# The prompt's state products moved to the head of each block of short products

## The chip, the core and the metric

The kernel runs on one core of one Trainium2 chip. The metric is the device time of one execution in microseconds (us). Engines: PE multiplies matrices, DVE (VectorE) and ACT (ScalarE) work on elements, POOL (GpSimd) does a little arithmetic and issues DMAs, SP (SyncE) issues DMAs. Each engine takes its instructions from a queue of its own and waits on semaphores for the others.

## The reference, cut to what matters

One layer of a hybrid streaming encoder for 256 rows of a new stream and 128 rows (8 streams of 16) of running ones, all in float32: one long projection, a pooling branch, a state-space branch (SSD), gates, an output projection and an MLP. The change lies in the SSD branch, which runs over 8 groups g of 8 heads:

```python
xbc, new_conv = causal_conv(xbc, st_conv, conv_w, conv_b)        # x, B, C after a short convolution
def step(h, inp):                                                # one chunk
    cum = cumsum(dtc * A);  decay = exp(cum[t] - cum[s])  (s <= t)
    cb = einsum('btgn,bsgn->btsg', Cc, Bc)
    y = einsum('btsgr,bsgrp->btgrp', cb * decay, xdt)            # within the chunk
    y = y + einsum('btgn,bgrpn->btgrp', Cc, h) * exp(cum)        # from the carried state
    h = h * exp(last) + einsum('bsgn,bsgr,bsgrp->bgrpn', Bc, w_end, xdt)   # the new state
y = y + d_skip * xh
a_ssd = rmsnorm_per_group(y * silu(z)) * g
```

For the prompt the carried state is zero, so its new state h is one product of B with the weighted x (x times dt times w_end) over all 256 rows. That product is "the state product of the prompt" in what follows. `rmsnorm_per_group` needs the sum of squares of a whole group.

## The kernel before, in words

**Tiles.** Rows lie along the free dimension: 384 columns, of which 256 are prompt and 128 are sample. A projection unit is 128 output channels: 16 k-steps of three products of 128x384, made in `half` (two halves of 8 k-steps, each with one weight tile of 128x1024). The three products per k-step (`mm3`, L76 to L78) replace one float32 product: each operand is split into a rounded high half and a rest. L76 is high weight by high input, L77 high weight by low input, L78 low weight by high input. A weight tile is loaded by SP (`wfetch`), its high half `wh` is made on ACT (L68) and its low half `wl` on DVE (L69, `wsplit`). There are three buffers for each of the three.

**One round per group** (loop at L799) is ten projection units: B, C, x0, x1, x2, x3, z0, z1, z2, z3. On PE they run in this order. Two blocks of short products stand between them:

- the first block, behind x2 (L834 to L847): `t_trx` (six transpositions of x0 and x1, tile trx, L587), `t_cb` (C by B, tile cb), `t_trB` (three transpositions of B, tile trB, L571), then for the previous group's second pair of channel tiles `t_pp` (six products, the state product of the prompt, tile py or pp, L630), `t_yT` and `t_Y` (tile Y), then `t_yi` for the new pair (tile py, L595) and `t_su` in `state` (the sample's new state, tile su, L735);
- the second block, behind z3 (L871 to L879): `t_trx` of x2 and x3, `t_pp`, `t_yT`, `t_Y` of the first pair, `t_yi` of the second pair, `t_su`.

In group 0 the first block has no part of a previous group; after group 7 the second pair's remainder runs behind the first unit of gate_b (L805 to L809). So there are 15 blocks in which `t_pp` stands between other short products, and one, after the last group, in which it stands directly behind long products.

The six products of `t_pp` multiply the split B (`Bhl`) with the split weighted x (`xhl`), both of type fp32r, as are the long products. Transpositions, cb, Y and yi are float32. `t_pp` writes the left half of a PSUM tile, `t_yi` the right half of the same tile. That tile comes from the pool `psm` of two buffers, which also holds the outputs of the long projections; all other short products write tiles of the pool `pss` of six.

**What reads the short products.** `bside` makes Bhl from trB (ACT L643, DVE L644); `xside` makes xdt and xdw from trx (four DVE instructions, L673), yis (L680) and xhl (ACT L687, DVE L688); `mside` makes cbm from cb (L666); `final` copies the state out (ACT L753), adds Y to x (L759) and multiplies by z (L767). An x unit is evicted from PSUM at L529 (then convolved, L540, L544), a z unit at L856 (then silu on ACT, L857).

**Between z1 and z2**, from group 1 on, `finish(prev)` (L865) normalizes the previous group: `norm_bc` splits the sum of squares (ACT L161, DVE L162 `nl`), sums it over the channels with two products on PE (tile bc, L165 and L166), and DVE takes the reciprocal root from it (L168, then `newton`, L151 to L155), after which L780 scales four tiles and POOL stores them.

**What sets the order.** On PE the order of this stage is written out: `half` and `lump` chain every group of products behind the last one (`tc.issue_after`). The queues of DVE, ACT, SP and POOL are not written out. A planner lays them when the kernel is built: it goes by the data each instruction needs, by its own estimates of how long things take, and by the order of the program. So the queue of one engine can be laid differently when the order on another engine is changed.

Of the kernel before, what the change touches and what calls it, by code (L numbers as in the profile page):

```python
# [33 lines left out]
def build(ctx, tc, io):  # L34
# [15 lines left out]
    def mmtile(name):  # L50
        return psm.tile([P, 512], F32, tag="mm", name=name)

    def sstile(name):
        return pss.tile([P, 512], F32, tag="ss", name=name)

    def behind(ins):
        return nullcontext() if ins is None else tc.issue_after(ins.ins)
# [440 lines left out]
    def gate_b(nb, pool, tag, hook=None):  # L498
        o = three(f"pj_gb{nb}")
        n = NB * 256 if tag == "hs" else 1536  # L500
        t = pool.tile([P, n], F32, tag=tag, name=f"gbt{nb}")[:, :1536].rearrange("p (b n) -> p b n", b=3)

        def done(b):
            s.activation(t[:, b], o[b], AF.Sigmoid, scale=yx[:, b : b + 1])
            gp.dma_start(gb_scr[nb][:, b], t[:, b])

        moving(o, [(io["w_gb"][nb, kp], f"gb{nb}_{kp}") for kp in range(8)], xg, 0, done, hook=hook)

    with tc.tile_pool(name="phd", bufs=2, reuse_waits="tile") as pd, tc.tile_pool(
# [40 lines left out]
        def lump(fn):  # L550
            with behind(last[0]):
                last[0] = fn()
# [3 lines left out]

        def pload(S):
            S.hs = pd.tile([P, NB, 2 * P], F32, tag="hs", name=f"hs{S.nm}")
            sy.dma_start(S.hs, io["ssm"][S.qd])

        def cload(S):
            S.cbcs = []
            for q in range(2):
                cbc = pd.tile([P, 2, T], F32, tag="cbc", name=f"cbc{S.nm}_{q}")
                sy.dma_start(cbc, cum_scr[S.h0 + q * 2 : S.h0 + q * 2 + 2, :].partition_broadcast(P))
                S.cbcs.append(cbc)
# [15 lines left out]
        def t_trx(S):  # L582
            S.trs = []
            for j in S.js:
                tr = sstile(f"trx{S.g}_{j}")
                for b in range(3):
                    i = te.transpose(tr[:, b * P : b * P + P], S.D.xs[j][:, b * P : b * P + P], ident)  # L587
                S.trs.append(tr[:, :T].rearrange("p (b h q) -> p b h q", b=3, h=2))
            return i
# [14 lines left out]
        def t_yT(S):  # L604
            S.Ys = []
            for q in range(2):
                Y = sstile(f"Y{S.nm}_{q}")
                i = te.transpose(Y[:, TP:T], S.yis[:, q], ident)
                S.Ys.append(Y)
            return i  # L610

        def t_Y(S):
            for q, Y in enumerate(S.Ys):
                for sb, e0, c0, n in ((0, 0, 0, TP), (1, TP, P, P), (2, T, TP, P)):
                    for c in range(4):
                        i = te.matmul(
                            Y[c * 32 : c * 32 + 32, c0 : c0 + n],
                            S.xdt[:, q, sb, c * 32 : c * 32 + 32],
                            S.E[:, q * 2 + c // 2, e0 : e0 + n],
                            start=False,  # L620
                            stop=sb > 0,
                            skip_group_check=True,
                        )
            return i

        def t_pp(S, py):
            S.pp = py[:, :256]
            for b in range(2):
                for bl, xl in ((0, 0), (0, 1), (1, 0)):
                    i = te.matmul(  # L630
                        S.pp.rearrange("p (j n) -> p j n", j=2),
                        S.D.Bhl[:, bl, b, :],
                        S.xhl[:, xl, :, b, :],
                        start=b + bl + xl == 0,
                        stop=b + bl == 2,
                        skip_group_check=True,
                    )
            return i
# [61 lines left out]
        def eside(S, q):  # L700
            if q == 0:
                S.E = pd.tile([P, 4, 512], F32, tag="E", name=f"E{S.nm}", bufs=1)
            for hh in (q * 2, q * 2 + 1):
                ch = S.cbcs[q][:, hh % 2]
                s.activation(S.E[:, hh, P:TP], ch[:, P:TP], AF.Exp, bias=tok[:, 9, S.h0 + hh : S.h0 + hh + 1])
                for b, e0 in enumerate((0, TP, T)):
                    s.activation(
                        S.E[:, hh, e0 : e0 + P],
                        ch[:, b * P : b * P + P],
                        AF.Relu,  # L710
                        bias=tok[:, b, S.h0 + hh : S.h0 + hh + 1],
                        scale=-1.0,
                    )
            Eq = S.E[:, q * 2 : q * 2 + 2]
            s.activation(Eq[:, :, :P], Eq[:, :, :P], AF.Exp, scale=-1.0)
            s.activation(Eq[:, :, TP:], Eq[:, :, TP:], AF.Exp, scale=-1.0)
            v.tensor_tensor(Eq, Eq, S.D.cbm.unsqueeze(1).to_broadcast([P, 2, 512]), ALU.mult)

        def dside(S):
            v.tensor_tensor(  # L720
                S.hs.rearrange("p b (h q) -> p b h q", h=4),
                S.hs.rearrange("p b (h q) -> p b h q", h=4),
                decb[:, S.h0 : S.h0 + 4, :].rearrange("p h b -> p b h").unsqueeze(3).to_broadcast([P, NB, 4, 64]),
                ALU.mult,
            )
# [72 lines left out]
        prev = None  # L798
        for g in range(G + 1):  # L799
            if g == G:  # L800
                eside(prev.p[1], 0)
                eside(prev.p[1], 1)
                dside(prev.p[1])
                gate_b(0, pd, "hs")
                py = mmtile("pp_last")  # L805
                lump(lambda: t_pp(prev.p[1], py))
                lump(lambda: t_yT(prev.p[1]))
                lump(lambda: t_Y(prev.p[1]))
                state(prev.p[1])  # L809
                final(prev.p[1])  # L810
                gate_b(1, pd, "hs")
                finish(prev)
                break
            u0 = 17 + g * 10
            D = Pair()
            D.g = g
            D.p = [pair(D, jp) for jp in range(2)]
            D.xs, D.zs = [], []
            D.BT = conv(u0, 32 + g, "BT", 2)
            pload(D.p[0])  # L820
            if g:
                eside(prev.p[1], 0)
            D.CT = conv(u0 + 1, 40 + g, "CT", 2)
            if g:
                eside(prev.p[1], 1)
            D.xs.append(conv(u0 + 2, g * 4, "xs", 6))
            if g:
                dside(prev.p[1])
            cload(D.p[0])
            cside(D)  # L830
            D.xs.append(conv(u0 + 3, g * 4 + 1, "xs", 6))
            b2 = conv_in(u0 + 4, g * 4 + 2)
            S = D.p[0]
            lump(lambda: t_trx(S))  # L834
            lump(lambda: t_cb(D))
            lump(lambda: t_trB(D))
            bside(D)
            S.py = mmtile(f"py{S.nm}")
            if g:
                lump(lambda: t_pp(prev.p[1], S.py))  # L840
                lump(lambda: t_yT(prev.p[1]))
                lump(lambda: t_Y(prev.p[1]))
            lump(lambda: t_yi(S))
            xside(S)
            mside(D)
            if g:
                state(prev.p[1])  # L847
                final(prev.p[1])
            D.xs.append(taps(b2, g * 4 + 2, "xs", 6))
            D.xs.append(conv(u0 + 5, g * 4 + 3, "xs", 6))  # L850
            eside(S, 0)

            def zproj(j):
                ps = proj(in_units(u0 + 6 + j), xg, f"z{g}_{j}")
                z = pd.tile([P, T], F32, tag="zs", name=f"zs{g}_{j}", bufs=7)
                v.tensor_tensor(z, ps, rstd, ALU.mult)  # L856
                s.activation(z, z, AF.Silu)  # L857
                D.zs.append(z)

            zproj(0)  # L860
            pload(D.p[1])
            eside(S, 1)
            zproj(1)
            if g:
                finish(prev)  # L865
            zproj(2)
            dside(S)
            cload(D.p[1])
            zproj(3)
            S1 = D.p[1]  # L870
            lump(lambda: t_trx(S1))  # L871
            S1.py = mmtile(f"py{S1.nm}")
            lump(lambda: t_pp(S, S1.py))
            lump(lambda: t_yT(S))
            lump(lambda: t_Y(S))
            lump(lambda: t_yi(S1))
            xside(S1)
            state(S)
            final(S)  # L879
            prev = D  # L880
# [311 lines left out]
    with tc.tile_pool(name="phg", bufs=1, reuse_waits="tile") as pg, tc.tile_pool(  # L1192
# [9 lines left out]
        for c8 in range(NC):  # L1202
            hh = []
            for f8 in range(8):
                f = c8 * 8 + f8
# [167 lines left out]
```

## Time and profile before

| | |
|---|---|
| median of 3 runs | 2807.32 us (2806.77 to 2808.29) |
| profiled execution | 2807.07 us |
| its span, first to last instruction | 2804.9 us |
| PE busy | 2792.9 us (100%) |
| DVE busy | 1501.4 us (54%) |
| ACT busy | 1173.4 us (42%) |
| the groups' stage, from the first block to the last | about 483 to 1237 us of the span |

In rows of the profile, L77 is line 77 of the kernel, `py<-xhl,Bhl` an output and its inputs, x6 a count of instructions. In a timeline a row shows the start, the length and the engine, and in brackets how long the engine had been idle before and what released it. A product's length includes its way through the array, so products overlap: what one costs is read from start to start.

### The profile page before, as it was taken

The numbers are of one execution on the slowest core, as the hardware profiler recorded it, in microseconds if no ns is written. First come the engines' busy times: TensorE is split into PE (matmuls) and PEld (weight loads), VectorE is DVE, ScalarE is ACT, GpSimd is POOL, SyncE is SP. The second block draws the span as 40 slices with busy tenths as digits, with TensorE's granted clock in tenths as the row PEclk, the third lists the DMA queues.
The fourth block names the chain that finished last, engine by engine and source line by source line (L and its number), as shares of the span: only waits on it lengthen the run. The fifth ranks groups of instructions, "written<-read, shape, count | busy, mean of one in ns | idle before, by whom it ended". The sixth has DMA issues, their size and how long they took to land.

```text
span 2804.9 us, 38300 instructions
## 1 busy us (share of the span) xinstructions
PE 2792.9 (100%) x15271; PEld 2542.6 (91%) x15271; DVE 1501.4 (54%) x1979; ACT 1173.4 (42%) x1822; POOL 105.8 (4%) x143
## 2 busy tenths in 40 slices
PE   9999999999999999999999999999999999999998
PEld 8998889999999999988888888989899898989897
DVE  6575335677787778756333336434444444444446
ACT  5443225556565656544322235433233332323233
POOL 0000000001010101010000000000000000000000
PEclk9999999999999999999999999999999999999999
DMA  7444445556665566657544544443444443444443
GB/s 272 131 124 150 139 139 199 186 182 207 197 228 192 201 198 223 197 186 233 175 146 161 176 144 131 130 131 125 131 126 129 127 130 126 129 128 128 130 127 124
DMA packets 148355, 451.35 MB, mean 161 GB/s; under 512 B 18064, under 2 KB 49104, under 8 KB 143184
## 3 DMA queue, kind: packets, MB, share of 16 engines
q1 hardware_dynamic: 140048, 412.97, 45.9%
q0 software_dynamic: 8128, 35.93, 3.3%
q8 instruction: 120, 1.97, 0.3%
q14 instruction: 59, 0.48, 0.1%
HBM read 407.11 MB, written 41.72 MB: 160 GB/s over the span
## 4 chain that ended last, share of the span: by engine, by line
PE 98%; ACT 1%; DMA 0%; DVE 0%; issue 0%; SPq 0%; DVEq 0%; ACTq 0%
PE pj_up L77 6%; PE pj_up L78 6%; PE pj_up L76 6%; PE wd L120 6%; PE wd L118 6%; PE wd L119 6%; PE pj_x L76 5%; PE pj_x L78 4%; PE pj_x L77 4%; PE pj_z L76 3%; PE pj_z L77 3%; PE pj_z L78 3%; PE pj_sp L119 3%; PE pj_sp L120 3%; PE pj_sp L118 3%; PE pj_gb L118 2%
## 5 line engine op out<-in xcount | busy, mean ns | idle before, releaser
L77 PE MATMUL pj_up<-x1l,wh_up 128*128 128x384 f32 (+1 forms) x1032 | 343.9, 333 | 0.6 <-DVE x1l L1041 0.6
L76 PE MATMUL pj_up<-x1h,wh_up 128*128 128x384 f32 (+1 forms) x1032 | 344.0, 333 | 0.0
L78 PE MATMUL pj_up<-x1h,wl_up 128*128 128x384 f32 (+1 forms) x1032 | 343.9, 333 | 0.0
L120 PE MATMUL wd<-wh_wd,hl 128*128 128x512 f32 x762 | 296.6, 389 | 0.0
L119 PE MATMUL wd<-wl_wd,hh 128*128 128x512 f32 x762 | 296.6, 389 | 0.0
L118 PE MATMUL wd<-wh_wd,hh 128*128 128x512 f32 x762 | 296.3, 389 | 0.0
L69 DVE TENSOR_TENSOR wl_wd<-w_wd,wh_wd 128x1024 fp32r<-128x1024 f32 x127 | 155.7, 1226 | 261.9 <-ACT wh_wd L68 261.9
L68 ACT ACTIVATE wh_wd<-w_wd 128x1024 fp32r<-128x1024 f32 x127 | 134.8, 1061 | 350.8 <-PE wd L120 284.2
L68 ACT ACTIVATE wh_up<-w_up 128x1024 fp32r<-128x1024 f32 x126 | 133.7, 1061 | 322.1 <-PE pj_up L77 258.0
L69 DVE TENSOR_TENSOR wl_up<-w_up,wh_up 128x1024 fp32r<-128x1024 f32 x126 | 154.4, 1226 | 198.1 <-ACT wh_up L68 198.0
L76 PE MATMUL pj_x<-xgh,wh_x 128*128 128x384 f32 x768 | 258.2, 336 | 0.0
L77 PE MATMUL pj_x<-xgl,wh_x 128*128 128x384 f32 x768 | 256.6, 334 | 0.0
L78 PE MATMUL pj_x<-xgh,wl_x 128*128 128x384 f32 x768 | 256.6, 334 | 0.0
L77 PEld LDWEIGHTS pj_up<-x1l,wh_up 128*128 128x128 f32 x1032 | 193.8, 188 | 1.0 <-DVE x1l L1041 0.7
L76 PEld LDWEIGHTS pj_up<-x1h,wh_up 128*128 128x128 f32 x1032 | 193.7, 188 | 0.3
L78 PEld LDWEIGHTS pj_up<-x1h,wl_up 128*128 128x128 f32 x1032 | 193.8, 188 | 0.0
L78 PE MATMUL pj_z<-xgh,wl_z 128*128 128x384 f32 x512 | 171.0, 334 | 0.0
L76 PE MATMUL pj_z<-xgh,wh_z 128*128 128x384 f32 x512 | 171.0, 334 | 0.0
L77 PE MATMUL pj_z<-xgl,wh_z 128*128 128x384 f32 x512 | 171.0, 334 | 0.0
L120 PEld LDWEIGHTS wd<-wh_wd,hl 128*128 128x128 f32 x762 | 143.0, 188 | 29.8
L119 PEld LDWEIGHTS wd<-wl_wd,hh 128*128 128x128 f32 x762 | 143.0, 188 | 29.7
L118 PEld LDWEIGHTS wd<-wh_wd,hh 128*128 128x128 f32 x762 | 143.0, 188 | 29.4
(319 smaller groups left out, 5799.7 us busy)
## 6 DMA issues: line engine op xcount, KB each, us to landing
w_up<-w_up SPq DMA_DIRECT2D x128, 512.0 KB, 3.4
w_wd<-w_down SPq DMA_DIRECT2D x128, 512.0 KB, 3.4
w_x<-w_in SPq DMA_DIRECT2D x96, 512.0 KB, 3.8
w_z<-w_in SPq DMA_DIRECT2D x64, 512.0 KB, 3.9
w_sp<-w_ssd SPq DMA_DIRECT2D x64, 512.0 KB, 3.4
w_ga<-w_ga SPq DMA_DIRECT2D x32, 512.0 KB, 3.5
w_pp<-w_pp SPq DMA_DIRECT2D x32, 512.0 KB, 3.4
hs<-ssm SPq DMA_DIRECT2D x16, 1024.0 KB, 5.4
```

The source lines that it names most:

```text
L68: s.activation(h, w, AF.Copy)
L69: v.tensor_tensor(l, w, h.bitcast(F32), ALU.subtract)
L76: te.matmul(out, wh, xh, start=first, stop=False, **how)
L77: te.matmul(out, wh, xl, start=False, stop=False, **how)
L78: return te.matmul(out, wl, xh, start=False, stop=last, **how)
L118: te.matmul(o[b], mh, wh[:, c], start=k == 0, stop=False)
L119: te.matmul(o[b], mh, wl[:, c], start=False, stop=False)
L120: last[0] = te.matmul(o[b], ml, wh[:, c], start=False, stop=k == nk - 1)
```

## The change

In the first block the PSUM tile of the new pair is taken, and `t_pp` of the previous group's second pair is issued, ahead of `t_trx`, `t_cb` and `t_trB`. In the second block the tile is taken and `t_pp` is issued ahead of `t_trx`. No instruction is added or removed, and no operand changes. Behind L834 the lines of the new kernel are numbered one higher (the eviction of z is L857 there, its silu L858).

```diff
             S = D.p[0]
+            S.py = mmtile(f"py{S.nm}")
+            if g:
+                lump(lambda: t_pp(prev.p[1], S.py))
             lump(lambda: t_trx(S))
             lump(lambda: t_cb(D))
             lump(lambda: t_trB(D))
             bside(D)
-            S.py = mmtile(f"py{S.nm}")
             if g:
-                lump(lambda: t_pp(prev.p[1], S.py))
                 lump(lambda: t_yT(prev.p[1]))
                 lump(lambda: t_Y(prev.p[1]))
             lump(lambda: t_yi(S))
...
             S1 = D.p[1]
-            lump(lambda: t_trx(S1))
             S1.py = mmtile(f"py{S1.nm}")
             lump(lambda: t_pp(S, S1.py))
+            lump(lambda: t_trx(S1))
             lump(lambda: t_yT(S))
             lump(lambda: t_Y(S))
             lump(lambda: t_yi(S1))
```

## The prediction

> **What bounds the kernel now.** I read the page first. The span is 2804.9 us; with 2.17 us around it the profiled execution took 2807.07 us, 0.25 us under the median of the three runs (2807.32). My sum is made against the 2807.07.
>
> ```profile
> span 2804.9 us, 38300 instructions
> PE 2792.9 (100%) x15271; PEld 2542.6 (91%) x15271; DVE 1501.4 (54%) x1979; ACT 1173.4 (42%) x1822; POOL 105.8 (4%) x143
> PEclk9999999999999999999999999999999999999999
> PE 98%; ACT 1%; DMA 0%; DVE 0%; issue 0%; SPq 0%; DVEq 0%; ACTq 0%
> ```
>
> PE is on the chain of work for 98% and its granted clock never falls, so any time the changed kernel gains or loses must appear as PE issuing its products closer together or further apart. The waits listed for PE say whether there is an idle stretch to win back; there are four in the whole span, and the only one that hits a block of short products is this, in the very first block, which has no state product yet:
>
> ```profile
> PE trx L587 <- ACT xs L544: 0.5, 1, 0.5
> ```
>
> So there is no wait in the 15 blocks that the change touches. Next the timeline of PE through a second block of a round (start, length, line, output<-inputs, count):
>
> ```profile
> 718.98 0.34 PE L78 MATMUL pj_z<-xgh,wl_z 128*128 128x384 f32 x1
> 719.16 0.82 PE L587 MATMUL trx<-cst,xs 128*128 128x128 f32 x6
> 719.73 0.96 PE L630 MATMUL py<-xhl,Bhl 128*128 128x256 f32 x6
> 720.53 0.38 PE L608 MATMUL Y<-cst,yis 128*128 128x128 f32 x2
> ...
> 723.61 0.74 PE L735 MATMUL su<-xst,bst 64*128 64x256 f32 x8
> 724.28 0.45 PE L76 MATMUL pj_x<-xgh,wh_x 128*128 128x384 f32 x1
> ```
>
> From the last long product to the next it takes 724.28 - 718.98 = 5.30 us, without a gap.
>
> **Part 1, the order on PE.** The six state products (py, L630) now stand behind the long product, and the transpositions behind them. Today the transpositions hold PE 719.73 - 719.16 = 0.57 us and the state products 720.53 - 719.73 = 0.80 us, 1.37 together. What the new neighbours cost is seen where the order already exists, after the last group, and in a first block:
>
> ```profile
> 1233.21 0.39 PE L120 MATMUL pj_gb<-wh_gb,xgl 128*128 128x512 f32 x1
> 1233.44 0.88 PE L630 MATMUL pp_last<-xhl,Bhl 128*128 128x256 f32 x6
> 1234.15 0.38 PE L608 MATMUL Y<-cst,yis 128*128 128x128 f32 x2
> ```
>
> ```profile
> 575.52 0.81 PE L587 MATMUL trx<-cst,xs 128*128 128x128 f32 x6
> 576.18 1.04 PE L577 MATMUL cb<-xs,xs 128*128 128x256 f32 x6
> 577.06 0.49 PE L571 MATMUL trB<-cst,xs 128*128 128x128 f32 x3
> 577.30 0.95 PE L630 MATMUL py<-xhl,Bhl 128*128 128x256 f32 x6
> 578.10 0.38 PE L608 MATMUL Y<-cst,yis 128*128 128x128 f32 x2
> ```
>
> Directly behind long products the six take 1234.15 - 1233.44 = 0.71 us; six transpositions followed by work of their own type take 576.18 - 575.52 = 0.66. Second block: 0.71 + 0.66 = 1.37, today 1.37. First block: three trB and the six take 578.10 - 577.06 = 1.04 today; then 0.71 + 3 x 0.11 = 1.04. The change of operand type costs the state products 0.09 us and gives as much back to the transpositions in front, so the new order is worth nothing. Bounds: the whole 0.09 won or lost in each of 15 blocks, 1.3 us, 0.05% either way. I take 0.
>
> The first state product must find its PSUM buffer free and its operands made. In the second block the buffer is that of z_2, evicted (L856) some 8 us earlier; the operands come from the block before, over 40 us back. No wait, cost 0.
>
> **Part 2, what is moved without being named in the diff.** Only PE's order is written out in this stage. The queues of DVE, ACT, SP and POOL are laid by the planner from its own estimates, and the built kernel shows that it lays them differently around every block. I compared for each product on PE how many products lie between it and the last PE work that its operands' queue must wait for. Today no product of this stage depends on an operand whose queue waits for PE work fewer than 12 products back. In the changed kernel there are seven places, one in each of groups 1 to 7, where it is 3: the first use of the low half of z_2's first weight tile (L78). The DVE queue from z_0's eviction on, group 1 (zs is the eviction, wl the making of a low half, nl, ssum, ny, na the norm of the group before):
>
> ```
> before: wl_z_1_0, E, nl, zs_0, wl_z_1_1, wl_z_2_0, zs_1, wl_z_2_1, ssum(L168), wl_z_3_0, ny(L151), na(L153) ...
> after:  wl_z_1_0, wl_z_1_1, E, zs_0, nl, zs_1, ssum(L168), ny(L151), na(L153), wl_z_2_0, na(L154), wl_z_2_1 ...
> ```
>
> zs_1 waits for the end of z_1 on PE, and z_2 comes right behind z_1. Today wl_z_2_0 is made during z_1; then it is made after z_1 has ended, behind four other instructions. That DVE does not step past a waiting instruction is in today's trace:
>
> ```profile
> 698.03 1.06 ACT L68 ACTIVATE wh_z<-w_z 128x1024 fp32r<-128x1024 f32 x1 [0.97 <-PE pj_z L77]
> ```
>
> ```profile
> 696.15 2.36 DVE L69 TENSOR_TENSOR wl_z<-w_z,wh_z 128x1024 fp32r<-128x1024 f32 x2 [1.54 <-ACT wh_z L68]
> 702.37 0.56 DVE L856 TENSOR_TENSOR zs<-pj_z,rstd 128x384 f32<-128x384 f32 x1 [3.86 <-PE pj_z L78]
> 702.84 1.22 DVE L69 TENSOR_TENSOR wl_z<-w_z,wh_z 128x1024 fp32r<-128x1024 f32 x1
> 703.97 0.55 DVE L168 TENSOR_SCALAR ssum<-bc_g 128x384 f32<-128x384 f32 x1
> 704.47 1.23 DVE L69 TENSOR_TENSOR wl_z<-w_z,wh_z 128x1024 fp32r<-128x1024 f32 x1
> 705.61 0.35 DVE L151 TENSOR_SCALAR ny_g<-ssum 128x384 int32<-128x384 int32 x1
> 706.00 0.56 DVE L153 TENSOR_TENSOR na_g<-ny_g 128x384 f32<-128x384 f32 x1
> 706.59 0.56 DVE L154 TENSOR_TENSOR na_g<-na_g,ssum 128x384 f32<-128x384 f32 x1
> ...
> 710.75 0.56 DVE L153 TENSOR_TENSOR na_g<-ny_g 128x384 f32<-128x384 f32 x1
> 711.23 0.55 DVE L856 TENSOR_TENSOR zs<-pj_z,rstd 128x384 f32<-128x384 f32 x1
> ```
>
> The high half of z_2_1 was ready at 699.09, yet its low half was made at 702.84, behind the eviction that waited for PE. Here that costs nothing, as z_2_1 is needed half a projection later. Now PE at the same place:
>
> ```profile
> 702.00 0.33 PE L78 MATMUL pj_z<-xgh,wl_z 128*128 128x384 f32 x1
> 702.17 0.33 PE L165 MATMUL bc_g<-nh_g,onesr 128*128 128x384 f32 x1
> 702.34 0.33 PE L166 MATMUL bc_g<-nl_g,onesr 128*128 128x384 f32 x1
> 702.52 0.33 PE L76 MATMUL pj_z<-xgh,wh_z 128*128 128x384 f32 x1
> ...
> 702.86 0.33 PE L78 MATMUL pj_z<-xgh,wl_z 128*128 128x384 f32 x1
> ```
>
> The walk, clock 0 at z_1's last product (702.00). zs_1 starts at 0.37, as today. The next independent DVE instruction starts 0.47 later (702.84 - 702.37): L168 at 0.84; its input, the second bc product, starts at 0.34 and is readable 0.37 after that, so at 0.71. L151 needs L168's result: 0.84 + 0.55 + 0.04 = 1.43 (0.04 is what lies between L151's end, 705.96, and L153). L153 at 1.43 + 0.39 = 1.82. wl_z_2_0 needs nothing of L153 and starts 0.48 later (711.23 - 710.75), at 2.30; at 1.23 it ends at 3.53. PE wants it at 702.86 - 702.00 = 0.86. How PE takes up after a wait for DVE is seen once:
>
> ```profile
> 1739.62 0.35 DVE L1041 SCALAR_TENSOR_TENSOR x1l<-trl,vec,x1h 128x128 fp32r<-128x128 f32 x1 [1.18 <-ACT x1h L1035]
> ```
>
> ```profile
> 1740.03 0.33 PE L77 MATMUL pj_up<-x1l,wh_up 128*128 128x128 f32 x1 [0.57 <-DVE x1l L1041]
> 1740.19 0.28 PE L78 MATMUL pj_up<-x1h,wl_up 128*128 128x128 f32 x1
> 1740.31 0.27 PE L77 MATMUL pj_up<-x1l,wh_up 128*128 128x128 f32 x1
> ```
>
> 0.06 us from DVE's end (1739.97) to PE's start, and the next spacing is 0.16 instead of 0.12, 0.04 more. So z_2's third product comes at 3.59 instead of 0.86 and the stage is 2.73 + 0.04 = 2.77 us later. Nothing covers this: all that PE could do is queued behind that product. Bounds: had wl_z_2_0 come directly behind zs_1 (0.84, end 2.07) the wait would be 1.31 us; if L168, L151 and L153 each started only after the whole of the one before, and the split after L153's end at 2.38, it would end at 3.61 and the wait be 2.85. I take 2.77, since each of its steps has its own row.
>
> Does it end there? wl_z_2_1, two instructions on, starts near 3.9 and ends near 5.1; its first use is 24 products of 0.173 after 3.59, at 7.75. wl_z_3_0 and wl_z_3_1 follow with several us to spare. The wait is paid once a group and not passed on.
>
> **Part 3, the blocks themselves.** The planner also puts a split in front of the four xside instructions (L673): in the second block wl_x_0, the first half for C. Its high half needs ACT:
>
> ```profile
> 719.23 1.06 ACT L68 ACTIVATE wh_x<-w_x 128x1024 fp32r<-128x1024 f32 x1 [3.10 <-PE pj_z L77]
> ```
>
> Clock 0 at 718.98: that ends at 1.31, the split runs from 1.34 and its successor starts 1.13 later (703.97 - 702.84), at 2.47; four xside at 0.47 end at 2.47 + 3 x 0.47 + 0.55 = 4.43. The second pair of su products takes over their PSUM buffers at 723.61 - 718.98 + 0.34 = 4.97. 0.5 us to spare: cost 0. The first block by the same rows: split, two xside, a third, Bhl, the fourth, cbm; the last ends near 5.5 against 6.2 for su. Cost 0. If the cover of 0.5 us were missed, each 0.1 us of it would cost 0.1 us in 8 blocks. On SP the weight loads now stand ahead of the small stores and reloads of xst and bst, which have over 40 us until su: 0; POOL's moved stores feed nothing of the stage: 0.
>
> **Sum.** 2807.07 + 0 (order) + 7 x 2.77 (19.4) + 0 (blocks) = 2826.5 us, 0.7% more. About 0.2%, 5.6 us, is what a measurement of this kernel can tell from no change.
>
> **Rivals.** (a) The clock of PE falls after each wait. On today's side: the granted clock is full in all slices, and behind the 0.57 us wait the products went on at 0.16 and 0.12 us; but no wait of today is as long as these, 2.6 us from the end of the second z_2 product (0.69 + 0.33 = 1.02) to 3.59. If the rest of z_2's first half ran at half speed, 22 products would cost another 22 x 0.173 = 3.8 us a group: 2826.5 + 27 = 2853; for half as long, 2840. [...]
>
> (b) Not slower: the wait is covered. For this the split would have to be finished by 0.86, which it is only if DVE is free to make it before z_1 ends, as today; the point from which it decides is a wait of 0.8 us a group (5.6 / 7). DVE has 3.86 us of idle time there to do it in, but the in-order row at 702.84 speaks against its being used. Then only part 1 is left: 2807.1, at best 2805.8.
>
> (c) The blocks lose too: the 0.5 us of cover in the second block is missed by up to 0.5 us, say because ACT starts the high half late. 8 x 0.5 = 4 us: 2830.5.
>
> **Chances.** Forecast 0.80, with a range of its own of 2823 to 2829 (2.5, a tenth under the walk, to 2.85 us a group, and part 1's 1.3 us either way); (c) 0.07, (a) 0.07, (b) 0.06. The range is 2818 to 2836: down to 1.6 us a group, near the 1.31 bound, and up past (c) towards the small end of (a). Of (b), 0.02 is left for a gain over 5.6 us, for which I see no mechanism, and the rest is the same time: faster 0.02, same 0.04, slower 0.94.
>
> **What would show it.** PE waits of about 2.6 us in front of z_2's third product (L78) released by DVE wl_z L69, seven times, none in group 0; a z_2 stretch 2.8 us longer while both kinds of block keep 5.3 and 6.5 us from long product to long product; all stages after group 7 the same. Wrong would be: blocks of other lengths, waits of 1.3 us or under, products behind the wait spaced at 0.35 us, or no wait at z_2 at all.

## The result and the profile after

The changed kernel takes 2834.09 us (median; 2832.49 to 2834.29) beside 2807.63 us of the kernel before on the same chip (2806.77 to 2808.29): a ratio of 1.0092 with a 95% interval of 1.008 to 1.0104. It is 26.5 us slower. The forecast was 19.4 us slower, 2826.5 us; the time lies inside the range of 2818 to 2836 and outside the forecast's own range of 2823 to 2829. The profiled execution took 2834.29 us, 0.2 us over the median, so its rows can be set against the 2807.07 us of the profiled execution before: 27.2 us more.

The page of the changed kernel, its first lines and the chain:

```profile
span 2832.5 us, 38292 instructions
PE 2802.4 (99%) x15271; PEld 2550.4 (90%) x15271; DVE 1505.3 (53%) x1979; ACT 1174.1 (41%) x1822; POOL 123.7 (4%) x143
...
PE 84%; issue 12%; ACT 1%; DMA 1%; DVE 1%; POOL 0%; SPq 0%; DVEq 0%; POOLq 0%; ACTq 0%
```

PE issues the same 15271 products. Its busy time rose from 2792.9 to 2802.4 us, 9.5 us, and its idle time (span less busy time) from 12.0 to 30.1 us, 18.1 us. So there are two losses of different kinds: PE waits, and PE is longer at the same products. The chain's "issue 12%" is not a third. Its long pieces lie between 101 and 443 us, ahead of the loop over the groups, where the page's slices show PE busy for 90% or more, as before: the chain only found nothing to follow there.

The waits of PE name the first loss, in the first row of that view (total us, times, longest us):

```profile
PE pj_z L78 <- DVE wl_z L69: 17.8, 7, 2.5
```

That is the predicted wait, seven times, in front of the third product of z_2 in groups 1 to 7, where the kernel before had none. The last product of z_1 on PE in group 1, and the timeline of DVE behind it, show the walk of the prediction happening (start, length, engine, line, operation, out<-in; in brackets the idle time before and its releaser):

```profile
607.24 0.33 PE L78 MATMUL pj_z<-xgh,wl_z 128*128 128x384 f32 x1
```

```profile
607.61 0.56 DVE L857 TENSOR_TENSOR zs<-pj_z,rstd 128x384 f32<-128x384 f32 x1 [6.59 <-PE pj_z L78]
608.09 0.55 DVE L168 TENSOR_SCALAR ssum<-bc_g 128x384 f32<-128x384 f32 x1
608.67 0.36 DVE L151 TENSOR_SCALAR ny_g<-ssum 128x384 int32<-128x384 int32 x1
609.07 0.56 DVE L153 TENSOR_TENSOR na_g<-ny_g 128x384 f32<-128x384 f32 x1
609.54 1.22 DVE L69 TENSOR_TENSOR wl_z<-w_z,wh_z 128x1024 fp32r<-128x1024 f32 x1
```

DVE sits idle for 6.59 us, then five instructions stand in a row, and the last of them is the split that PE needs. PE meanwhile, in group 1 and then in group 2:

```profile
607.93 0.34 PE L77 MATMUL pj_z<-xgl,wh_z 128*128 128x384 f32 x1
610.81 0.69 PE L78 MATMUL pj_z<-xgh,wl_z 128*128 128x384 f32 x1 [2.54 <-DVE wl_z L69]
611.30 0.52 PE L76 MATMUL pj_z<-xgh,wh_z 128*128 128x384 f32 x1
611.62 0.52 PE L77 MATMUL pj_z<-xgl,wh_z 128*128 128x384 f32 x1
```

```profile
707.48 0.34 PE L77 MATMUL pj_z<-xgl,wh_z 128*128 128x384 f32 x1
710.36 0.44 PE L78 MATMUL pj_z<-xgh,wl_z 128*128 128x384 f32 x1 [2.54 <-DVE wl_z L69]
710.63 0.33 PE L76 MATMUL pj_z<-xgh,wh_z 128*128 128x384 f32 x1
710.81 0.34 PE L77 MATMUL pj_z<-xgl,wh_z 128*128 128x384 f32 x1
```

The wait is 2.54 us in both. What follows is not the same. In group 2 the products go on 0.18 us apart; in group 1 they are 0.32 us apart and last 0.52 instead of 0.33 us. That is the second loss. The stretches around both waits (window, its length, then busy us and, in brackets, the instructions that touch the window, of PE, PEld, DVE, ACT and POOL, the granted clock of PE, the share of the DMA engines, GB/s):

```profile
607.31:610.72 3.41, 0.96 (x6) 0.64 (x4) 3.04 (x6) 2.42 (x3) 0.00 (x0) 1.00 0.00 0
610.72:614.13 3.41, 3.32 (x10) 3.32 (x11) 3.41 (x6) 0.00 (x0) 0.00 (x0) 0.50 0.56 169
614.13:617.54 3.41, 3.41 (x21) 3.41 (x21) 2.71 (x6) 1.06 (x1) 0.00 (x0) 1.00 0.81 274
```

```profile
706.29:709.71 3.42, 1.53 (x9) 1.21 (x7) 2.48 (x5) 1.96 (x3) 0.00 (x0) 1.00 0.00 0
709.71:713.12 3.41, 2.76 (x16) 2.77 (x17) 3.41 (x5) 0.46 (x1) 0.00 (x0) 1.00 0.43 154
```

For exactly one stretch of 3.41 us PE was granted half its clock: 10 products where the next stretch holds 21. This happened in five of the seven groups (stretches from 610.72, 808.69, 907.68, 1105.65 and 1204.64 us), and not behind the waits at 707.5 and 1004.6 us.

The sum closes. From one group's first block to the next one's, the kernel before takes 95.25 us. The changed one takes 98.05 in the two groups without a half-clock stretch, 2.80 more, and 99.45 to 99.6 in those with one, on average 4.30 more (four groups; the seventh has no next first block and is taken as these). 2 x 2.80 + 5 x 4.30 = 27.1 us, of the 27.2 that the execution is longer. Of these, 7 x 2.80 = 19.6 us are the wait and 5 x 1.50 = 7.5 us the clock.

The blocks, where the change was made, kept their lengths. PE through a second block of the changed kernel, from its last long product in front to the first one behind:

```profile
628.55 0.33 PE L78 MATMUL pj_z<-xgh,wl_z 128*128 128x384 f32 x1
628.73 0.88 PE L630 MATMUL py<-xhl,Bhl 128*128 128x256 f32 x6
629.44 0.82 PE L587 MATMUL trx<-cst,xs 128*128 128x128 f32 x6
630.10 0.38 PE L608 MATMUL Y<-cst,yis 128*128 128x128 f32 x2
...
633.85 0.44 PE L76 MATMUL pj_x<-xgh,wh_x 128*128 128x384 f32 x1
```

633.85 - 628.55 = 5.30 us, as before. The state products hold PE 629.44 - 628.73 = 0.71 us instead of 0.80, and the transpositions 630.10 - 629.44 = 0.66 instead of 0.57: what one gains by its new neighbour the other loses, 1.37 us together in both kernels.

### The profile page after: what moved, and what is told of

Read it like the earlier page. It is cut to its first block, busy times and chain, and to the rows that moved or that the text cites. A ratio compares the mean times of both kernels' runs of the same rounds, so it can differ in the third digit from the quotient of the medians.

```text
span 2832.5 us, 38292 instructions
## 1 busy us (share of the span) xinstructions
PE 2802.4 (99%) x15271; PEld 2550.4 (90%) x15271; DVE 1505.3 (53%) x1979; ACT 1174.1 (41%) x1822; POOL 123.7 (4%) x143
## 4 chain that ended last, share of the span: by engine, by line
PE 84%; issue 12%; ACT 1%; DMA 1%; DVE 1%; POOL 0%; SPq 0%; DVEq 0%; POOLq 0%; ACTq 0%
PE pj_up L77 6%; PE pj_up L78 6%; PE pj_up L76 6%; PE wd L119 6%; PE wd L120 6%; PE wd L118 6%; PE pj_x L76 4%; PE pj_x L78 4%; PE pj_x L77 4%; PE pj_z L78 3%; PE pj_z L76 3%; PE pj_z L77 3%; PE pj_sp L119 3%; PE pj_sp L118 3%; PE pj_sp L120 3%
```

## The experiments

The theory after the result: the new order on PE is worth nothing by itself; all of the loss is the split of z_2's first low half being late, 2.80 us a group, and the clock that falls behind five of the seven waits. Rivals: the other things that the planner laid anew on DVE, SP and POOL cost something too; the extra time behind the waits is PE's way of taking up work and not the idle time as such.

### The split put back in front

In the changed kernel, z_1's eviction and the first step of the norm are told to queue behind the split of z_2's first low half. PE's order is that of the changed kernel.

```diff
-        v.tensor_tensor(l, w, h.bitcast(F32), ALU.subtract)
+        low[name] = v.tensor_tensor(l, w, h.bitcast(F32), ALU.subtract)
...
-        v.tensor_scalar(hm, o, -0.5 / n, -0.5 * EPS, ALU.mult, ALU.add)
+        with behind(low.get(f"z{int(name[1:]) + 1}_2_0")):
+            v.tensor_scalar(hm, o, -0.5 / n, -0.5 * EPS, ALU.mult, ALU.add)
...
-                v.tensor_tensor(z, ps, rstd, ALU.mult)
+                with behind(low.get(f"z{g}_2_0") if j == 1 else None):
+                    v.tensor_tensor(z, ps, rstd, ALU.mult)
```

> The changed kernel, with one thing put back on DVE: from group 1 on, z_1's eviction and the norm's first instruction (L168) are queued behind the split of z_2's first low half. All the other re-laid queues stay as in the changed kernel. Theory (the loss is only the wait for that split, 7 x 2.8 us, and the half clock behind it, 5 x 1.5 us): 2807 us, within 1.5 us of the kernel before, no PE wait in the z_2 stretch, blocks still 5.3 and 6.5 us. Rival (part of the loss, the 7.6 us that the waits do not explain, comes from other re-laid queues): 2814 to 2815 us.

Measured: 2807.17 us (2806.85 to 2808.24) beside 2807.64 of the kernel before, ratio 0.9999 (0.999 to 1.0009). Its waits of PE, from the first row on, and its row of cores (span, mean granted clock):

```profile
PE warm_o L204 <- POOL warm L200: 1.3, 1, 1.3
PE pj_up L79 <- DVE x1l L1046: 0.6, 1, 0.6
PE pj_p L78 <- ACT wh_e L262: 0.4, 1, 0.4
```

```profile
core 0: 2804.8 us, clock 0.999
```

No wait at z_2 is left and the span is that of the kernel before (2804.9). Two queue positions on DVE take back all 26.5 us. PE's and POOL's orders are those of the changed kernel here, and by the traces (buffer numbers left out) under ten rows each on ACT and SP and some 35 of 1979 on DVE stand elsewhere, so nearly all else that the planner laid anew is still in place. It costs nothing that this comparison of 0.1% can tell, and the moved state products gain nothing.

### A wait of 1.1 us

Of the two instructions queued behind the split above only the norm's first step stays there, and z_1's eviction stays where the planner put it: the split then comes second behind z_1's end, not fifth.

```diff
-        v.tensor_tensor(l, w, h.bitcast(F32), ALU.subtract)
+        low[name] = v.tensor_tensor(l, w, h.bitcast(F32), ALU.subtract)
...
-        v.tensor_scalar(hm, o, -0.5 / n, -0.5 * EPS, ALU.mult, ALU.add)
+        with behind(low.get(f"z{int(name[1:]) + 1}_2_0")):
+            v.tensor_scalar(hm, o, -0.5 / n, -0.5 * EPS, ALU.mult, ALU.add)
```

> The changed kernel with only L168 queued behind the split of z_2's first low half: the split then follows z_1's eviction directly. Theory (the wait is what DVE does between z_1's end and the split's end; the clock falls only behind long gaps): a wait of 1.3 to 1.4 us a group, PE idle for 1.1 us in it, no product behind it at half speed; 2807.1 + 7 x 1.35 = 2816.5 us. Rival (the clock falls behind any such wait, or the rest has another cause): another 7.6 us, 2824 us.

Measured: 2816.4 us (2815.94 to 2816.72), ratio 1.0031 (1.0018 to 1.0043). Its row of waits, and PE in group 1:

```profile
PE pj_z L80 <- DVE wl_z L69: 7.6, 7, 1.1
```

```profile
607.28 0.34 PE L79 MATMUL pj_z<-xgl,wh_z 128*128 128x384 f32 x1
608.70 0.44 PE L80 MATMUL pj_z<-xgh,wl_z 128*128 128x384 f32 x1 [1.08 <-DVE wl_z L69]
608.98 0.33 PE L78 MATMUL pj_z<-xgh,wh_z 128*128 128x384 f32 x1
```

The loss is 2816.4 - 2807.6 = 8.8 us. From start to start the gap is 608.70 - 607.28 = 1.42 us instead of 0.17, and 0.1 us goes at the next product: 1.35 x 7 = 9.5, which is 0.7 over the measured loss. The mean granted clock, 0.999 over 2814.4 us, is that of the kernel before; a half-clock stretch of 3.41 us behind each of the seven waits would take 7 x 1.7 / 2814.4 = 0.004 off it. These seven waits of 1.1 us cost their own length and nothing more.

### The gap filled with work

Twelve more products of 128x384 are put in front of z_2's first product in groups 1 to 7. They write z_2's own PSUM tile, which z_2's first product then starts over, so the kernel computes what it did and PE does 84 products more. The wait for the split ends when it ended; only PE is no longer idle for most of it.

```diff
-    def proj(units, rhs, name):
+    def proj(units, rhs, name, fill=0):
...
-            half(o, q, take(src, f"{name}_{q}"), rhs)
+            wl_ = take(src, f"{name}_{q}")
+            if fill and q == 0:
+                with behind(last[0]):
+                    for _ in range(fill):
+                        last[0] = te.matmul(o, wl_[0][:, :P], rhs[0][0], start=True, stop=True)
+            half(o, q, wl_, rhs)
...
-                ps = proj(in_units(u0 + 6 + j), xg, f"z{g}_{j}")
+                ps = proj(in_units(u0 + 6 + j), xg, f"z{g}_{j}", 12 if g and j == 2 else 0)
```

> The changed kernel with 12 more products of 128x384 on PE ahead of z_2's first one, in groups 1 to 7; they write z_2's own PSUM tile and are overwritten by its first product, so this is added work of 12 x 0.173 = 2.08 us that lies inside the wait. Theory: the split is ready when it was, z_2's third product starts at the same time, PE is idle for 0.5 us instead of 2.5, and nothing runs at half speed behind it: 2807.1 + 7 x 2.8 = 2826.7 us, under the changed kernel though PE does more. Rival (the 7.6 us are not the clock): 2834 us.

Measured: 2826.29 us (2825.78 to 2826.57), ratio 1.0068 (1.0053 to 1.0083). PE in group 1 of this kernel (the twelve products are the first row), and its cores:

```profile
607.55 2.24 PE L111 MATMUL pj_z<-xgh,wh_z 128*128 128x384 f32 x12
609.63 0.33 PE L76 MATMUL pj_z<-xgh,wh_z 128*128 128x384 f32 x1
609.80 0.34 PE L77 MATMUL pj_z<-xgl,wh_z 128*128 128x384 f32 x1
610.60 0.44 PE L78 MATMUL pj_z<-xgh,wl_z 128*128 128x384 f32 x1 [0.46 <-DVE wl_z L69]
```

```profile
core 0: 2824.5 us, clock 0.999
```

With 84 products more the kernel is 2834.09 - 2826.29 = 7.8 us faster than the changed one, and the mean granted clock is 0.999 again, where the changed one has 0.996. This parts the two losses cleanly. What remains, 2826.29 - 2807.64 = 18.7 us, is the lateness of the split, 0.9 less than the trace's 19.6. What went, 7.8 us, is what PE's idleness costs beyond the wait, as the trace had it (5 x 1.50 = 7.5). The time is also within 0.2 us of the predicted one: what the forecast described is this kernel with the clock kept up.

### Each block's move alone

From the kernel before, once the move in the second block alone and once that in the first block alone.

```diff
-            lump(lambda: t_trx(S1))
             S1.py = mmtile(f"py{S1.nm}")
             lump(lambda: t_pp(S, S1.py))
+            lump(lambda: t_trx(S1))
```

> The kernel before with the move made in the second block alone. There z_2's first low half stays queued ahead of z_1's eviction. Theory (the place of the state product on PE is worth nothing, the loss hangs on the re-laid DVE queue): 2807 us, within 1.5 us. Rival (the move itself costs or gains on PE): off by 8 x up to 0.09 us = 0.7 us, too little to tell, or more if DVE's later start in the second block is felt, up to 4 us.

Measured: 2807.15 us (2806.45 to 2810.13), ratio 1 (0.9991 to 1.0009). The second block takes 1010.44 - 1005.15 = 5.29 us:

```profile
1005.15 0.33 PE L78 MATMUL pj_z<-xgh,wl_z 128*128 128x384 f32 x1
...
1009.78 0.74 PE L735 MATMUL su<-xst,bst 64*128 64x256 f32 x8
1010.44 0.44 PE L76 MATMUL pj_x<-xgh,wh_x 128*128 128x384 f32 x1
```

DVE inside that block:

```profile
1006.49 1.23 DVE L69 TENSOR_TENSOR wl_x<-w_x,wh_x 128x1024 fp32r<-128x1024 f32 x1 [0.41 <-ACT wh_x L68]
...
1009.03 0.55 DVE L673 TENSOR_TENSOR xdw<-trx,tok 128x384 f32<-128x384 f32 x1
```

The split in front of the xside instructions is there, as predicted, and the last of them ends at 1009.03 + 0.55 = 1009.58; the second pair of su products, which takes over their PSUM buffers, comes near 1009.78 + 0.34 = 1010.1. The cover of half a microsecond holds.

```diff
             S = D.p[0]
+            S.py = mmtile(f"py{S.nm}")
+            if g:
+                lump(lambda: t_pp(prev.p[1], S.py))
             lump(lambda: t_trx(S))
             lump(lambda: t_cb(D))
             lump(lambda: t_trB(D))
             bside(D)
-            S.py = mmtile(f"py{S.nm}")
             if g:
-                lump(lambda: t_pp(prev.p[1], S.py))
                 lump(lambda: t_yT(prev.p[1]))
```

> The kernel before with the move made in the first block alone. There the DVE queue has z_2's first low half behind z_1's eviction and the norm's first steps, as in the changed kernel. Theory: all of the loss, 2834 us (7 waits of 2.8 us and some 5 stretches at half speed). Rival (the second block's move has a share): less, by up to half, 2820 us.

Measured: 2833.47 us (2832.9 to 2834.29) beside 2806.6, ratio 1.0094 (1.0076 to 1.0112). Its waits of PE have the same first row as the changed kernel, and four of its seven waits are followed by a half-clock stretch. So the move of six products in the first block alone makes the planner put the split behind z_1's eviction, further on in the group; the move in the second block does not. Why the planner does so isn't settled: the estimates from which it laid the queues are in none of these records. Nor is the whole size: by the terms above, 7 x 2.80 + 4 x 1.50 = 25.6 us, 1.3 less than the 26.9 measured.

This kernel also gives one more case of the clock, the stretch of a wait and the one after it:

```profile
1200.19:1203.60 3.41, 1.44 (x9) 1.12 (x7) 2.56 (x5) 2.04 (x3) 0.00 (x0) 1.00 0.02 8
1203.60:1207.00 3.40, 2.83 (x9) 2.83 (x10) 3.40 (x5) 0.38 (x1) 0.00 (x0) 0.50 0.47 157
```

### A wait twice as long

In the changed kernel the split of z_2's first low half is put off further, behind the first step of the norm's root.

```diff
-        v.tensor_tensor(l, w, h.bitcast(F32), ALU.subtract)
+        rest = lambda: v.tensor_tensor(l, w, h.bitcast(F32), ALU.subtract)
+        if name.startswith("z") and name.endswith("_2_0") and name != "z0_2_0":
+            deferred.append(rest)
+        else:
+            rest()
...
             if g:
                 finish(prev)
+                with behind(steps[-3]):
+                    deferred.pop()()
             zproj(2)
```

> The changed kernel with the split of z_2's first low half put further back on DVE, behind the norm's first root step, z_2's second low half and one more step. By the rows of before it ends at 6.3 us after z_1's last product, a wait of 5.5 us a group with 5.3 us of PE idle: 2807.1 + 7 x 5.55 = 2846 us from the wait alone. Theory (the clock falls at the end of a stretch of 3.4 us in which PE was mostly idle): all 7 waits show half speed, part of it hidden in the idle time, 0 to 1.7 us each: 2846 to 2858 us. Rival (a fixed 7.6 us of another cause): 2854 us with products behind the waits at full speed.

Measured: 2859.26 us (2857.33 to 2862.23), ratio 1.0186 (1.017 to 1.0202), 1.3 us above the top of what was expected. Its row of waits and the stretches of group 1:

```profile
PE pj_z L84 <- DVE wl_z L69: 37.3, 7, 5.3
```

```profile
608.75:612.16 3.41, 0.00 (x0) 0.00 (x0) 3.31 (x6) 1.74 (x2) 0.00 (x0) 1.00 0.00 0
612.16:615.57 3.41, 2.10 (x7) 2.10 (x8) 3.38 (x6) 0.00 (x0) 0.00 (x0) 0.50 0.71 209
615.57:618.99 3.42, 3.42 (x12) 3.42 (x12) 3.31 (x7) 0.00 (x0) 0.77 (x2) 0.50 0.71 256
```

Now every wait, 5.33 us, is followed by half clock, each time for two stretches in a row, and the mean granted clock is 0.990 over 2860.5 us. The wait alone would make 7 x 5.6 = 39.2 us; the loss is 2859.26 - 2806.6 = 52.7, so the clock takes 13.5 us, 1.9 a group. That is less than two full stretches would cost, since the first begins while PE is still idle: in group 1 at 612.16, with PE's next product at 613.47.

## Why the prediction was right and where it was wrong

Part 1, the order on PE, taken at 0 with bounds of 1.3 us either way: right, and borne out by the two kernels that have a new order without a wait, at ratios of 0.9999 (both blocks) and 1 (second block). Their intervals of 0.1%, 2.5 us, are wider than the bounds; the trace of the first is finer, 95.22 us from group to group beside 95.25 before.

Part 2, the split behind z_1's eviction: right in place, count and size. With z_1's last product at 607.24 as clock 0, the four instructions and the split start at 0.37, 0.85, 1.43, 1.83 and 2.30, where the walk had 0.37, 0.84, 1.43, 1.82 and 2.30; PE takes up at 3.57 where it had 3.59. The stage is 2.80 us later and not 2.77. That it does not pass the wait on holds too: in the two groups without half clock the 2.80 is all there is.

Part 3, the blocks at 0: right, 5.3 and 6.5 us as before, and the cover of the second block held. Rival (c) falls with it. Rival (b), a wait that is covered, falls by the seven waits: DVE's idle time in front of the eviction, 6.59 us, was there and wasn't used.

The step that failed is the term for the clock. The sum gave it nothing, and rival (a) had 0.07, on the ground that the products behind a wait of 0.57 us had gone on at full pace. That row could not bear a wait over four times as long, and the prediction said itself that none of that length was on record: that the clock stays up behind one was not shown. The term measures 7.5 us: half clock for one stretch of 3.41 us in five groups of seven, 1.50 us each. Rival (a) had the fall of the clock but not its size. Its 27 us took 22 products at half speed in each group; 8 to 11 were, and not in every group. One of the prediction's own signs of being wrong, products behind the wait spaced at 0.35 us, was nearly met: in those five groups they are 0.32 us apart. That the time still lies inside the wide range is owed to the range, which reached past rival (c), and not to the sum, which fell short by this term.

Of the 14 waits of 2.54 us in two kernels nine were followed by half clock. The five half-clock stretches of the changed kernel are each 3.413 us long in the clock records of its trace, and their starts lie 197.97, 98.99, 197.97 and 98.99 us apart, which are 58, 29, 58 and 29 times that length. So the clock fell behind gaps shorter than one such stretch, and in these 14 waits the fall went with how little PE did in the stretch of 3.41 us on which the gap happened to fall: 0.96 us ahead of the fall at 610.72, and 1.53 us ahead of 709.71, where the clock stayed up.

## What to carry to other kernels

When one engine's order is edited and others are laid by a planner, compare the built queues of all engines, and for each product count how much work lies between it and whatever its operand's queue waits for; here the moved products were worth nothing and a queue that no line of the diff names was worth the whole 26.5 us. Cost a new idle stretch of the product engine twice, by its length and by the clock behind it: in this kernel waits of 1.1 us cost their length, waits of 2.5 us nothing or about 1.5 us more, waits of 5.3 us about 1.9 us more. Where such a wait can't be removed, throwaway products in it can pay: 84 of them won back 7.8 us.

## What the runs showed of the hardware

That the clock falls behind waits of 2.54 us in some groups and not in others was not expected. PE's busy time is read here in stretches of 3.41 us, the measured length of a half-clock stretch, counted from where these begin. In the 14 waits of the changed kernel and of the one with the first block's move, a stretch in which PE was busy for 0.87 to 1.44 us was followed by half clock, nine times, and one with 1.53 us or more wasn't, five times. The stretches at both ends of that, 1.44 and 1.53, are above.

The clock returned after a half-clock stretch with PE busy for 2.83 us of it, and did not after one with 2.10 (the long wait, 612.16). At half clock a product took 0.32 us from start to start (611.30 to 611.62 in the changed kernel) instead of 0.173, so the busy times at the two clocks can't be compared as they stand. Estimated in products of this size, 1.44 and 1.53 us at full clock are 1.44 / 0.173 = 8.3 and 1.53 / 0.173 = 8.8, and 2.10 and 2.83 us at half clock are 2.10 / 0.32 = 6.6 and 2.83 / 0.32 = 8.8.

One stretch doesn't go with the busy times of the 14 waits. In the profiled execution with the long wait (2862.23 us, 3 us over the median) there was one more half-clock stretch far from any z wait, at the head of the up-projection:

```profile
1793.17:1796.58 3.41, 2.84 (x26) 2.70 (x25) 3.00 (x9) 3.38 (x12) 0.00 (x0) 1.00 0.00 0
1796.58:1799.99 3.41, 3.41 (x15) 3.41 (x15) 3.25 (x10) 1.69 (x7) 0.54 (x1) 0.50 0.19 36
```

PE was busy for 2.84 us ahead of it, though nearly all of the 26 were products of 128 columns, a third of the 384 that those in z have. The kernel with waits of 1.1 us has nearly the same stretch, counted back in lengths of 3.413 us from the fall of its clock at 2809.83 us, behind its last product. There the clock stayed up:

```profile
1748.29:1751.70 3.41, 2.84 (x26) 2.70 (x25) 2.67 (x8) 3.38 (x13) 0.00 (x0) 1.00 0.00 0
1751.70:1755.12 3.42, 3.42 (x26) 3.39 (x26) 3.42 (x11) 2.50 (x10) 0.54 (x1) 1.00 0.04 7
```

So neither PE's busy time nor the number of products that touch a stretch decides by itself: 2.84 us and 26 products stand ahead of the fall in the one kernel and ahead of no fall in the other. What exactly the clock goes by is shown by no run and stays open.
